# Overflow lists made in turns with the gate matrix, the last U blocks in the experts' pipeline, and the overflow pairs as the last row operations

## The chip, the cores and the metric

The kernel runs on one core of a Trainium2 chip. Its metric is the device time of one execution in microseconds (us). The engines are TensorE (PE, with PEld for its weight loads), VectorE (DVE), ScalarE (ACT), GpSimd (POOL) and SyncE (SP), which only issues transfers. Each engine works through its own list of instructions in order, and waits on semaphores for the others.

## The reference: what is computed

One encoder layer over 256 tokens of width 2048, in float32: a mix of retention and a gated recurrence, cross-attention over 256 memory tokens, then a feed-forward layer of 16384 experts of one neuron each ("PEER"), and a last normalisation. The change lies in the PEER part:

```
h = h + concat([retention, recurrence]) @ w_out
h = h + memory_cross_attention(...)
q = xn @ peer_w_q                      # 8 heads, two halves each
...                                    # top 16 of 128 keys in each half, top 16 of their 256 pairs
gate = softmax(top_sc)                 # 8 x 16 = 128 experts for each token, eid = 128*i1 + i2
act  = gelu(sum_d xn[t, d] * u_tab[eid[t, k], d])
out[t] = sum_k gate[t, k] * act[t, k] * v_tab[eid[t, k]]
```

`u_tab` and `v_tab` are 16384 x 2048 each, 134 MB a table.

## The kernel before, in words

**Dense weights.** A weight piece is 512 KB of float32, loaded by SP into `raw` (128 x 1024). ACT rounds it to `hi` (L119 or L1092), DVE subtracts to get the rest, `lo` (L120 or L1098), and PE multiplies hi by the activations' two parts and lo by one of them. So each weight piece takes one load, one ACT cast, one DVE subtraction and some 2.7 us of matmuls.

**The experts are split.** 96 x 128 experts (`RD` = 96) are computed densely, for all 256 tokens: 12 chunks (`NCH`) of 8 blocks of 128 experts. For each chunk, the U half makes the hidden values (8 blocks of two pieces, PSUM tile `U`, folded by DVE into `foldu`, gelu on ACT into `act`), a gate matrix zeroes what a token did not choose, and the V half multiplies 16 pieces into the output. The gate matrix is built by `gbuild`: for each four tokens DVE makes one-hot matrices `o` (L868, L871), ACT scales one of them with the gates (L874), PE multiplies them into `G` (L884), the result is copied to `gs` (L886), and each time 16 tokens are full, `gs` goes to DRAM as `gd` (L890, 768 KB, in pieces of 512 bytes). 64 such groups, 16 such transfers. `gs` has two buffers. Each chunk later reads its two halves of `gd` back as `raw<-gd` and multiplies (`prep`, or `prep_steps` with L1046).

**The other 32 x 128 experts are fetched by row.** `chosen` gathers, with indirect transfers of 1 MB issued by POOL (L1135), one U row or V row for each of 128 tokens into a ring of four tiles (`gat` x3 and `h[1]`). A U row is used by one DVE dot product with the normalised tokens (L1152), a V row by one DVE multiply-add into `hh` (`axpy`, L1160). 36 slots for each of the two token tiles: 72 dots and 72 axpys, three gathers ahead. `compact` (with matmuls `off` and `spill`) makes the lists. A token with more than 36 such experts has the rest in an overflow list; `spill` treats up to two of its entries (`OV`) for each partition: two gathers of U rows, two of `hn` (the normalised tokens), two dots, a one-hot matrix `oh` with the weights, two gathers of V rows, and 16 float32 matmuls of those rows with `oh` (L996). What overflows even that is worked off in `rest`, a branch that a flag guards.

**What sets the order.** Up to the sixth U chunk a scheduler orders the instructions of each engine; side work (`gbuild`, then `compact`) is fed in by a `Weave`, `wv`, which earns `rate` credits with each weight piece and spends them on the generator's steps. From there the pipeline `run(steps)` is written out by hand: raw loads six steps ahead, hi three, lo two. Its steps are V pieces, U pieces of the chunk that lies six further on (`LEAD`), and G steps (the gate product). The row operations of `chosen` are fed in by the same `Weave` at `RC`. Chunks 0 to 5 have V and U steps, chunks 6 to 10 V steps only; then `wv.drain()` issues the row operations that are left, `rest()` follows, and `v_final(11)` does the last chunk with the final normalisation.

## Time and profile before

| | |
|---|---|
| time, median of 3 runs | 2092.89 us (2092.3 to 2096.95) |
| the profiled execution: time, span | 2099.48 us, 2097.7 us |
| granted TensorE clock, mean | 0.993 |
| PE, DVE, ACT, POOL busy | 2030.7, 1698.7, 1039.0, 342.0 us |
| from DRAM, to DRAM | 541.99 MB, 18.87 MB |

The span runs from the first to the last instruction. "Busy" of PE counts stretches in which matmuls were in the array or queued for it. The profile's windows give, for any stretch, the busy time of each engine, the granted clock of TensorE and the share of time that the 16 DMA engines were busy; its lists of waits say what ended an engine's idle time; its timeline lists single instructions, runs of equal ones put together. Of this kernel's span, the stage with the gate matrix and the last scheduled U chunks ends at about 1249 us, chunks 0 to 5 of the hand-written pipeline run to about 1782 us, chunks 6 to 10 to 2038 us, and the rest is the drain, the last chunk and the output.

### The profile page before, as it was taken

To read this page: it belongs to the slowest core of one execution; us is meant where nothing else is said; L and a number is where in the kernel's file an instruction comes from. 1 tells how busy PE (TensorE), PEld (TensorE's weight loads), DVE (VectorE), ACT (ScalarE), POOL (GpSimd) and SP (SyncE) were. 2 spreads that over 40 slices of the span, in tenths; PEclk is the share of its full clock that TensorE was granted. 3 is DMA by queue.
4 is the path that set the end of the run, shared out by engine and by line. 5 is a ranking of instruction groups with operands and counts; after the bars stand their busy time and mean duration, and the time that the engine had idled before them with its cause. 6 is when DMAs were issued, how large, how long until landed. Compare 5 with 4: busy or idle time off the path is not lost.

```text
span 2097.7 us, 29005 instructions
## 1 busy us (share of the span) xinstructions
PE 2030.7 (97%) x10452; PEld 1721.0 (82%) x10452; DVE 1698.7 (81%) x2455; ACT 1039.0 (50%) x1600; POOL 342.0 (16%) x195
## 2 busy tenths in 40 slices
PE   8999999999999999999999989999999999989997
PEld 6888878888888888888889968888888888767785
DVE  6859866744554457999987779999999999989897
ACT  6565434544544455554578853444444444433334
POOL 0200021000000000000000002323333332445342
PEclk9999999999999999999999999999999999999999
DMA  8675646566654468555686579999999999999874
GB/s 283 236 233 171 218 134 184 172 191 190 184 170 141 143 188 283 170 182 179 192 275 192 171 242 371 389 382 400 362 354 358 351 378 409 375 371 391 315 263 157
DMA packets 155015, 542.92 MB, mean 259 GB/s; under 512 B 17136, under 2 KB 44400, under 8 KB 136560
## 3 DMA queue, kind: packets, MB, share of 16 engines
q1 hardware_dynamic: 132832, 400.48, 56.7%
q0 software_dynamic: 22032, 140.53, 16.9%
q8 instruction: 82, 1.34, 0.3%
q14 instruction: 69, 0.57, 0.1%
HBM read 541.99 MB, written 18.87 MB: 267 GB/s over the span
## 4 chain that ended last, share of the span: by engine, by line
PE 77%; DVE 14%; DMA 4%; issue 3%; ACT 1%; POOL 1%; ACTq 0%; DVEq 0%; SPq 0%; POOLq 0%
PE U L129 13%; PE wb L129 8%; PE U L131 7%; PE xc L171 6%; PE xc L172 6%; PE xc L174 6%; PE acc L956 5%; PE acc L953 5%; PE acc L954 5%; PE wb L131 4%; DVE lo L120 4%; PE G L884 2%; PE V L956 2%; PE V L953 2%; PE V L954 2%
## 5 line engine op out<-in xcount | busy, mean ns | idle before, releaser
L120 DVE TENSOR_TENSOR lo<-raw,hi 128x1024 fp32r<-128x1024 f32 x396 | 486.0, 1230 | 261.9 <-PE xc L174 118.8
L119 ACT CAST hi<-raw 128x1024 fp32r<-128x1024 f32 x396 | 415.3, 1050 | 301.2 <-PE xc L172 165.2
L1092 ACT CAST hi<-raw 128x1024 fp32r<-128x1024 f32 x272 | 283.9, 1049 | 265.6 <-PE acc L954 91.1
L129 PE MATMUL U<-xn,hi 128*128 128x512 f32 x1536 | 401.7, 398 | 7.8 <-ACT hi L119 6.1
L1098 DVE TENSOR_TENSOR lo<-raw,hi 128x1024 fp32r<-128x1024 f32 x272 | 328.2, 1221 | 35.0 <-issue 16.6
L129 PEld LDWEIGHTS U<-xn,hi 128*128 128x128 f32 x1536 | 277.8, 190 | 58.3 <-ACT hi L119 6.2
L1135 POOL DMA_INDIRECT gat<-in_Us_dram,idx x69 | 122.2, 1771 | 682.6 <-DVE gat L1152 424.5
L131 PEld LDWEIGHTS U<-xn,lo 128*128 128x128 f32 x1536 | 210.1, 190 | 18.3 <-DVE lo L120 2.3
L131 PE MATMUL U<-xn,lo 128*128 128x256 f32 x1536 | 218.5, 284 | 1.8 <-DVE lo L120 1.3
L1152 DVE SCALAR_TENSOR_TENSOR gat<-gat,h 128x2048 f32<-128x2048 f32 x69 | 157.7, 2285 | 0.0
L953 PE MATMUL acc<-hi,ah 128*128 128x512 f32 x384 | 150.7, 392 | 1.5 <-DVE foldu L937 1.5
L954 PE MATMUL acc<-hi,al 128*128 128x512 f32 x384 | 150.4, 392 | 0.0
L129 PE MATMUL wb<-hT,hi 128*128 128x512 f32 x448 | 119.8, 400 | 0.0
L956 PE MATMUL acc<-lo,ah 128*128 128x512 f32 x384 | 103.4, 391 | 4.9 <-DVE lo L120 3.4
L1135 POOL DMA_INDIRECT gat<-in_Vs_dram,idx x39 | 86.7, 2223 | 130.3 <-DVE hh L1160 112.7
L129 PE MATMUL wb<-xT,hi 128*128 128x512 f32 x368 | 93.4, 394 | 2.1 <-ACT hi L119 2.1
L129 PEld LDWEIGHTS wb<-hT,hi 128*128 128x128 f32 x448 | 81.3, 189 | 14.0
L1160 DVE SCALAR_TENSOR_TENSOR hh<-gat,coef,hh 128x2048 f32<-128x2048 f32 x39 | 91.5, 2346 | 0.1
L956 PEld LDWEIGHTS acc<-lo,ah 128*128 128x128 f32 x384 | 71.9, 188 | 21.8 <-DVE lo L120 4.7
L1135 POOL DMA_INDIRECT h<-in_Vs_dram,idx x33 | 70.7, 2144 | 108.3 <-DVE hh L1160 101.5
L953 PEld LDWEIGHTS acc<-hi,ah 128*128 128x128 f32 x384 | 72.5, 189 | 16.8 <-DVE foldu L937 1.8
L954 PEld LDWEIGHTS acc<-hi,al 128*128 128x128 f32 x384 | 72.6, 189 | 15.2
(411 smaller groups left out, 3654.4 us busy)
## 6 DMA issues: line engine op xcount, KB each, us to landing
raw<-in_U_dram SPq DMA_DIRECT2D x192, 512.0 KB, 4.9
raw<-in_V_dram SPq DMA_DIRECT2D x192, 512.0 KB, 7.9
raw<-in_w_xyg_dram SPq DMA_DIRECT2D x48, 512.0 KB, 4.5
raw<-in_w_qkv_dram SPq DMA_DIRECT2D x48, 512.0 KB, 4.2
raw<-in_w_xk_dram SPq DMA_DIRECT2D x32, 512.0 KB, 3.6
raw<-in_w_xv_dram SPq DMA_DIRECT2D x32, 512.0 KB, 4.2
raw<-in_w_out_dram SPq DMA_DIRECT2D x32, 512.0 KB, 4.2
raw<-in_w_xq_dram SPq DMA_DIRECT2D x32, 512.0 KB, 3.5
```

Of the source, the lines that this page charges most:

```text
L119: A.copy(hi, raw)
L120: V.tensor_tensor(lo, raw, hi.bitcast(F32), op=ALU.subtract)
L129: PE.matmul(pt, hi[:, ks], xt[:, kb, :], start=(kb == 0), stop=(kb == KB - 1))
L131: PE.matmul(pt[:, :T], lo[:, ks], xt[:, kb, :T], start=False, stop=False)
L171: PE.matmul(pt, xh, hi[:, w], start=(n == 0 and k == 0), stop=False)
L953: PE.matmul(pt, ah[:, c, t_], hi[:, w], start=(first and c == 0), stop=False)
L954: PE.matmul(pt, al[:, c, t_], hi[:, w], start=False, stop=False)
L956: PE.matmul(pt, ah[:, c, t_], lo[:, w], start=False, stop=(last and c == 7))
L1092: A.copy(his[t], raws[t])
L1098: V.tensor_tensor(los[t], raws[t], his[t].bitcast(F32), op=ALU.subtract)
L1135: G.indirect_dma_start(gat, None, a[tab], bass.IndirectOffsetOnAxis(ap=idx[tt][:, k:k + 1], axis=0), bounds_check=NS - 1, oob_is_err=False)
L1152: V.scalar_tensor_tensor(gat, gat, 1.0, h[0], op0=ALU.mult, op1=ALU.mult, accum_out=dots[tt, k0][:, k:k + 1])
```

## The change

1. `gbuild` and `compact` are fed in turns instead of one after the other (`turns`), at a rate of 2.35 instead of 1.9. Every second copy G to `gs` is made by DVE, the others by ACT (before: all by ACT). The 16 transfers `gd<-gs` are issued by POOL instead of SP. The ring's `gat` tiles are cleared by POOL at the end of `compact`, instead of by DVE later.
2. `CUT` = 2: of the sixth U chunk, only two of the eight blocks are made by `u_chunk` under the scheduler; the other 12 pieces and the first chunk's two G steps become steps 0 to 13 of the pipeline, which so has 284 weight steps instead of 272. The old `prep`, with its wave of small steps, is gone. The weave is drained before, and the two loads `hh<-hd` (1 MB each) are issued at step 8 of the pipeline.
3. The overflow pairs are no longer a side job of chunks 7 to 9. Their gathers follow the last row operations, in the same ring; the two dots come after the last axpy, the V rows are fetched after them, and the 16 matmuls are added to the last chunk: 12 to the PSUM tiles of the first three column groups, 4 to those of the last.

```
-RA, RB, RC = 1.1, 1.9, 1.17
+RA, RB, RC = 1.1, 2.35, 1.17
+CUT = 2
...
+        ring.extend(slot("ms", [P, D], f"gat{n}") for n in range(3))
+        for gat in ring:
+            G.memset(gat, 0.0)
+        ring.append(h[1])
+
+    def turns(one, two):
+        for x in one:
+            yield x
+            y = next(two, None)
+            if y is not None:
+                yield y
+        yield from two
...
-                A.copy(gs[:, :, g0:g0 + 4, :],
-                       pt[:, :4 * RD].rearrange("p (t c x) -> p c t x", t=4, x=8))
+                (V.tensor_copy if m % 2 else A.copy)(
+                    gs[:, :, g0:g0 + 4, :], pt[:, :4 * RD].rearrange("p (t c x) -> p c t x", t=4, x=8))
...
-                    nc.sync.dma_start(gd[:, :, tl, :].rearrange("q p t c -> p q t c"), gs)
+                    G.dma_start(gd[:, :, tl, :].rearrange("q p t c -> p q t c"), gs)
...
-    def u_chunk(i):
+    def u_chunk(i, blocks):
-        for c in range(8):
+        for c in blocks:
-            if i == LEAD - 1 and c == 2:
-                while "gbuild" not in done:
-                    wv.pump(3.0)
-                wave.append(prep(0))
-        flush()
...
         for t, step in enumerate(steps):
+            if t == 8:
+                for tt in range(TT):
+                    nc.sync.dma_start(hh[tt], hd[tt])
...
-    def chosen(blocks):
+    def chosen(blocks, tail=False):
+        extra = [lambda: fetch(next_gat(), a["Us"], NS, spl["i"][:, 0:1]),
+                 lambda: spill_x(1, next_gat()),
+                 lambda: fetch(next_gat(), a["Us"], NS, spl["i"][:, 1:2])] if tail else []
         for m in range(len(tasks) + AHEAD):
             if m < len(tasks):
                 f, tab, tt, k0, n, k = tasks[m]
                 held.append(rows(tab, tt, k0 + k))
+            elif extra:
+                held.append(extra.pop(0)())
...
+                    if tail and not dots_left:
+                        spill_x(0, h[0])
                 yield 2.2
+        if tail:
+            spill_dot(0, held[-3], h[0])
+            spl["v"] = [next_gat() for b in range(OV)]
+            yield 2.2
+            spill_dot(1, held[-1], held[-2])
+            yield 2.2
+            spill_rows()
+            spill_weights()
...
-    wv.add(gbuild())
-    wv.add(compact())
+    wv.add(turns(gbuild(), compact()))
...
-        u_chunk(i)
+        u_chunk(i, range(8 if i < LEAD - 1 else CUT))
+    wv.drain()
...
-    wv.add(chosen(blocks_of(0, 0, BASE) + blocks_of(1, 0, BASE)))
-    steps = []
+    wv.add(chosen(blocks_of(0, 0, BASE) + blocks_of(1, 0, BASE), True))
+    steps = woven(list(u_steps(LEAD - 1))[2 * CUT:], prep_steps(0), 6, 3)
```

**Where gate matrix and U chunk end, on PE.** G is a group of four tokens of the gate matrix, U a piece of the dense U half, `off` and `spill` are `compact`'s. Before:

```order
L884 MATMUL G<-o_10820,o_10818 128x96 x4
L884 MATMUL G<-o_10834,o_10832 128x96 x4
L884 MATMUL G<-o_10849,o_10847 128x96 x4
L884 MATMUL G<-o_10864,o_10862 128x96 x4
L884 MATMUL G<-o_10878,o_10876 128x96
L798 MATMUL off<-ct,tri 128x1
L799 MATMUL off<-ct,ones 128x1
L800 MATMUL off<-ct,tri 128x1
L884 MATMUL G<-o_10878,o_10876 128x96 x3
L831 MATMUL spill<-sel,own 128x12
L129 MATMUL U<-xn,hi 128x512 x7
L831 MATMUL spill<-sel,own 128x12
```

After, the last groups of G, and what follows them:

```order
L896 MATMUL G<-o_10949,o_10947 128x96 x2
L130 MATMUL U<-xn,hi 128x512
L896 MATMUL G<-o_10949,o_10947 128x96 x2
L132 MATMUL U<-xn,lo 128x256 x8
L130 MATMUL U<-xn,hi 128x512
L896 MATMUL G<-o_10963,o_10961 128x96 x2
L130 MATMUL U<-xn,hi 128x512
L896 MATMUL G<-o_10963,o_10961 128x96 x2
L130 MATMUL U<-xn,hi 128x512 x5
L132 MATMUL U<-xn,lo 128x256 x8
L130 MATMUL U<-xn,hi 128x512 x9
L132 MATMUL U<-xn,lo 128x256 x8
```

The stretch of G groups without U pieces between them is gone, and `compact`'s matmuls stand further ahead.

**The gate matrix's transfers, at the same place.** Before, on SP, `gd<-gs` among the U loads, and the first two loads of the gate matrix:

```order
L890 DMA gd<-gs 128x12x128
L112 DMA raw<-gd 128x1024
L112 DMA raw<-in_U_dram 128x1024
L890 DMA gd<-gs 128x12x128
L112 DMA raw<-in_U_dram 128x1024 x2
L890 DMA gd<-gs 128x12x128 x5
L1326 DMA hh_11282<-hd 128x2048
L890 DMA gd<-gs 128x12x128
L112 DMA raw<-gd 128x1024
L112 DMA raw<-in_U_dram 128x1024 x4
```

After, on POOL, from the clearing of the ring on (the gathers L1099 are row operations; the second one into `gat_9629` is the fifth gather):

```order
L856 MEMSET gat_9631 128x2048
L1099 DMA gat_9629<-in_Us_dram,idx 128x2048
L902 DMA gd<-gs 128x12x128
L1099 DMA gat_9630<-in_Us_dram,idx 128x2048
L1099 DMA gat_9631<-in_Us_dram,idx 128x2048
L1099 DMA h_4211<-in_Us_dram,idx 128x2048
L902 DMA gd<-gs 128x12x128 x14
L1099 DMA gat_9629<-in_Us_dram,idx 128x2048
L902 DMA gd<-gs 128x12x128
```

And after, on DVE, from the last copy to `gs` (L898) up to the second gate product (L1007), which needs the last of those transfers (L1116 is the dot, L987 the fold of a U block):

```order
L898 COPY gs<-G 128x12x32
L1059 TENSOR_TENSOR lo<-raw_11005,hi 128x1024
L987 TENSOR_TENSOR foldu<-U,foldu 128x256
L1059 TENSOR_TENSOR lo<-raw_11006,hi 128x1024
L1116 SCALAR_TENSOR_TENSOR gat_9630,dots<-gat_9630,h_4210 128x2048
L1007 TENSOR_TENSOR act_7481<-raw,act_7481 128x8x128
L987 TENSOR_TENSOR foldu<-U,foldu 128x256
L1059 TENSOR_TENSOR lo<-raw,hi 128x1024
L1116 SCALAR_TENSOR_TENSOR gat_9631,dots<-gat_9631,h_4210 128x2048
L1059 TENSOR_TENSOR lo<-raw,hi 128x1024
L987 TENSOR_TENSOR foldu<-U,foldu 128x256
L1007 TENSOR_TENSOR act_7481<-raw,act_7481 128x8x128
```

The last transfer of the gate matrix now stands on POOL behind a gather that waits for the first dot, which stands on DVE right ahead of the last copy; and the gate product that needs that transfer follows on DVE eleven rows behind the copy. Before, the transfer was SP's, behind nothing but loads.

**The drain, on DVE.** Before, from the last lo of the pipeline on (L1160 is the axpy, L120 the lo of the last chunk):

```order
L1098 TENSOR_TENSOR lo<-raw_11314,hi 128x1024
L1160 SCALAR_TENSOR_TENSOR hh_11283<-gat_11292,coef,hh_11283 128x2048
L120 TENSOR_TENSOR lo<-raw,hi 128x1024
L1160 SCALAR_TENSOR_TENSOR hh_11283<-gat_11293,coef,hh_11283 128x2048
L1230 TENSOR_REDUCE more<-fl 128x1
L1160 SCALAR_TENSOR_TENSOR hh_11283<-gat_11294,coef,hh_11283 128x2048
L1232 CAST many<-more 128x1
L120 TENSOR_TENSOR lo<-raw,hi 128x1024
L1160 SCALAR_TENSOR_TENSOR hh_11283<-h_4211,coef,hh_11283 128x2048
```

Four more axpys follow in turns with four more lo, up to the branch. After (L1124 axpy, L1195 the overflow pairs' dots, L121 the lo of the last chunk, L1205 their one-hot weights):

```order
L1124 SCALAR_TENSOR_TENSOR hh_10983<-gat_9631,coef,hh_10983 128x2048
L1059 TENSOR_TENSOR lo<-raw,hi 128x1024
L1124 SCALAR_TENSOR_TENSOR hh_10983<-h_4211,coef,hh_10983 128x2048
L1195 SCALAR_TENSOR_TENSOR gat_9629,od<-gat_9629,h_4210 128x2048
L1195 SCALAR_TENSOR_TENSOR gat_9631,od<-gat_9631,gat_9630 128x2048
L1217 TENSOR_REDUCE more<-fl 128x1
L121 TENSOR_TENSOR lo<-raw,hi 128x1024
L1200 TENSOR_TENSOR od<-od,spg 128x2
L1219 CAST many<-more 128x1
L121 TENSOR_TENSOR lo<-raw,hi 128x1024
L1205 TENSOR_SCALAR oh<-iota,spt,od 128x128 x2
```

One axpy instead of eight stands behind the pipeline's last lo; behind it two dots stand between the pipeline's last lo and the first lo of the last chunk, and the second of them reads a row whose gather can only be issued when the axpy into which `gat_9631` goes is done.

More of the change, by code (lines that the diff above doesn't have):

```diff
@@ L821, in compact @@
         spl["i"] = tp.tile([P, OV], I32, tag="spi", name="spi")
-        spl["g"] = tp.tile([P, 40], F32, tag="spg", name="spg")[:, :OV]
+        spl["g"] = tp.tile([P, 64], F32, tag="spg", name="spg")[:, :OV]
         for b in range(OV):
@@ L893, in gbuild @@
         done.add("gbuild")
[L895 to L928 removed]
+    ahs, spare = {}, {}
+    def u_chunk(i, blocks):
         act = acts[i] = tp.tile([P, 8, T], F32, tag="act", name=f"act{i}", bufs=LEAD)
[L930 removed]
+        for c in blocks:
             pt = mm("U") if i or c else pt0
@@ L961, in v_unit @@
         first, last = not kept or i == 0, not kept or i == NCH - 1
-        late = i == SPILL + 2
+        late = i == NCH - 1
         for q in range(4):
@@ L984, in products @@
                 if not box:
-                    if i == SPILL + 2:
-                        while side:
-                            for _ in side.pop():
-                                pass
                     box.extend(acc[dc] if kept else (mm("V0"), mm("V1")))
                 ah, al = ahs[i]
-                late = i == SPILL + 2
-                v_mms(ah, al, hi, lo, q, list(enumerate(box)), not kept or i == 0, not kept and not late)
-                if late and q == 3:
-                    for tt in range(TT):
-                        for b in range(OV):
-                            PE.matmul(box[tt], spl["oh"][:, b, tt * P:(tt + 1) * P],
-                                      spl["v"][b][:, dc * 512:(dc + 1) * 512], start=False,
-                                      stop=(not kept and b == OV - 1))
+                v_mms(ah, al, hi, lo, q, list(enumerate(box)), not kept or i == 0, not kept)
             def added(dc=dc, kept=kept, box=box):
@@ L1177, in chosen @@
         held = []
+        dots_left = sum(t[0] is dot for t in tasks)
+        extra = [lambda: fetch(next_gat(), a["Us"], NS, spl["i"][:, 0:1]),
+                 lambda: spill_x(1, next_gat()),
+                 lambda: fetch(next_gat(), a["Us"], NS, spl["i"][:, 1:2])] if tail else []
         for m in range(len(tasks) + AHEAD):
@@ L1222, in spill, with spill_rows @@
                 V.tensor_scalar(spl["t"][:, bs], spl["t"][:, bs], -float(P), None, op0=ALU.add)
-        yield
-        done.add("spill")
+    def spill_rows():
+        for b in range(OV):
+            fetch(spl["v"][b], a["Vs"], NS, spl["i"][:, b:b + 1])
     def rest():
@@ L1276, in v_final @@
             for q in range(4):
-                v_mms(ah, al, vl[:, q, 0], vl[:, q, 1], q, [(tt, pt)])
+                v_mms(ah, al, vl[:, q, 0], vl[:, q, 1], q, [(tt, pt)], last=False)
+            for b in range(OV):
+                PE.matmul(pt, spl["oh"][:, b, tt * P:(tt + 1) * P], spl["v"][b][:, ds], start=False,
+                          stop=(b == OV - 1))
             V.tensor_tensor(hh[tt][:, ds], hh[tt][:, ds], pt, op=ALU.add)
@@ L1318, in hybrid_layer_kernel @@
     done.add("pb")
-    wv.add(gbuild())
-    wv.add(compact())
+    wv.add(turns(gbuild(), compact()))
     wv.rate = RB
     for i in range(LEAD):
-        u_chunk(i)
+        u_chunk(i, range(8 if i < LEAD - 1 else CUT))
+    wv.drain()
     hh = [slot("qs", [P, D], f"hh{tt}") for tt in range(TT)]
-    for tt in range(TT):
-        nc.sync.dma_start(hh[tt], hd[tt])
-    wv.drain()
     pg.__exit__(None, None, None)
@@ L1333, in hybrid_layer_kernel @@
     pct = pc.__enter__()
-    ring = [slot("ms", [P, D], f"gat{n}") for n in range(3)] + [h[1]]
-    for gat in ring[:3]:
-        V.memset(gat, 0.0)
     pj = tc.tile_pool(name="pj", bufs=1, space=bass.MemoryType.PSUM)
```

83 lines of the change are left out of this document (22 added, 61 removed).

## The prediction

> **What bounds the kernel now.** I read the page's head and its chain first:
>
> ```profile
> span 2097.7 us, 29005 instructions
> PE 2030.7 (97%) x10452; PEld 1721.0 (82%) x10452; DVE 1698.7 (81%) x2455; ACT 1039.0 (50%) x1600; POOL 342.0 (16%) x195
> PE 77%; DVE 14%; DMA 4%; issue 3%; ACT 1%; POOL 1%; ACTq 0%; DVEq 0%; SPq 0%; POOLq 0%
> ```
>
> PE is busy in 97% of the span, so all that can be won without removing matmuls is 2097.7 - 2030.7 = 67 us of idle time and what the clock takes; and the change removes no matmul. So I looked for the places where PE stands, with the windows (length, busy time of PE, PEld, DVE, ACT, POOL, then the granted clock, the DMA share and GB/s):
>
> ```profile
> 1155.00:1209.00 54.00, 54.00 (x386) 50.18 (x384) 42.57 (x65) 48.06 (x142) 0.00 (x0) 1.00 0.56 173
> 1209.00:1220.00 11.00, 8.14 (x58) 7.18 (x58) 8.02 (x25) 10.36 (x33) 0.00 (x0) 1.00 0.51 146
> 1220.00:1249.00 29.00, 21.45 (x114) 18.63 (x114) 20.32 (x50) 12.81 (x19) 0.00 (x0) 0.82 0.86 318
> 1249.00:1782.00 533.00, 530.86 (x2683) 450.96 (x2682) 514.13 (x535) 235.19 (x303) 171.53 (x97) 1.00 0.96 371
> 1782.00:1826.00 44.00, 41.70 (x184) 33.60 (x183) 43.82 (x46) 19.48 (x21) 16.84 (x7) 1.00 0.95 371
> 1826.00:1900.00 74.00, 63.72 (x263) 49.39 (x262) 64.12 (x64) 22.11 (x23) 33.57 (x15) 0.98 0.95 381
> 1900.00:2038.00 138.00, 133.39 (x553) 103.15 (x553) 128.40 (x117) 53.66 (x56) 62.06 (x26) 1.00 0.87 321
> 2038.00:2062.00 24.00, 20.59 (x82) 15.81 (x81) 23.75 (x18) 7.29 (x10) 7.90 (x4) 0.93 0.56 184
> ```
>
> Four places count: the end of the gate matrix and of the scheduled U chunks (1209 to 1249, 10.4 us idle, clock down to 0.82), the V chunks without U (1782 to 2038, 17.2 us idle), the drain (3.4 us idle, clock 0.93), and, as a place that is full, chunks 0 to 5 (2.1 us idle in 533, so PE sets the pace, with DVE at 96% and DMA at 0.96 right behind). The waits name what PE stood for, up to 1782 us, and then from there on:
>
> ```profile
> PE U L129 <- ACT hi L119: 6.1, 1, 6.1
> PE spill L831 <- DVE own L817: 1.9, 1, 1.9
> PE acc L953 <- DVE foldu L937: 1.5, 1, 1.5
> ```
>
> ```profile
> PE acc L956 <- DVE lo L1098: 10.6, 10, 4.3
> PE acc L956 <- DVE lo L120: 3.4, 3, 2.2
> PE V L953 <- ACT hi L1092: 2.4, 3, 1.0
> ```
>
> The first three are the end of the gate matrix; lo L1098 is the V chunks, lo L120 the drain. Between 1826 and 1872 us ACT in its turn waits for the loads:
>
> ```profile
> ACT hi L1092 <- DMA raw<-in_V_dram: 19.9, 7, 5.2
> ```
>
> That is the chunk in which the overflow pairs' six 1 MB gathers run beside the row operations.
>
> **Step 1, the end of the gate matrix.** From 1209 to 1249 PE was busy for 8.14 + 21.45 of 40 us: 10.4 idle. Some matmuls behind the gaps were slow:
>
> ```profile
> 1220.01 3.06 PE L129 MATMUL U<-xn,hi 128*128 128x512 f32 x7
> 1233.93 3.70 PE L129 MATMUL U<-xn,hi 128*128 128x512 f32 x8 [6.08 <-ACT hi L119]
> 1238.41 1.78 PE L129 MATMUL U<-xn,hi 128*128 128x512 f32 x7
> ```
>
> Seven take 1.78 us at full clock, so the first row lost 1.3 us and the second 3.70 - 2.03 = 1.7. Excess of the stretch: 10.4 + 3.0 = 13.4 us. All of it hangs on the order that goes: G groups with no U pieces between, the lists behind them, then U pieces held by the first gate product. After, G and lists run among U pieces and the stage ends in the pipeline: -13.4.
>
> The Trainium skill, "TensorE: Matmul & The Clock Gate", Part 1 (The HAM clock gate), says that an idle window of about 3.4 us halves the clock and that as much sustained work restores it; the row after the 6.08 us gap agrees (8 matmuls at 3.70 us for 2.03). By it every new gap of that size would cost up to 1.7 us beyond its own length, and gaps of 1 or 2 us nothing; that would leave the sum where it is.
>
> What comes instead: the last `gd<-gs` stands on POOL behind the fifth gather, which waits for the first dot; the second gate product needs it, by way of SP's `raw<-gd`, which also holds the raw loads behind it. Prices:
>
> ```profile
> L886 ACT COPY gs<-G 128x384 f32<-128x384 f32 x64 | 29.8, 471 | 3.3 <-PE G L884 3.0
> L1135 POOL DMA_INDIRECT gat<-in_Us_dram,idx x69 | 122.2, 1771 | 682.6 <-DVE gat L1152 424.5
> 814.64 0.75 POOL L673 DMA_DIRECT2D hn<-h  x1 [485.63 <-DVE h L671]
> 817.23 0.57 POOL L673 DMA_DIRECT2D hn<-h  x1 [1.84 <-DVE h L671]
> gd<-gs SPq DMA_DIRECT2D x16, 768.0 KB, 5.3
> raw<-gd SPq DMA_DIRECT2D x24, 512.0 KB, 8.1
> L890 SPq DMA_DIRECT2D gd<-gs x16: 359/377/426, 1076.3 to 1218.5; - x16
> L1098 DVE TENSOR_TENSOR lo<-raw,hi 128x1024 fp32r<-128x1024 f32 x272 | 328.2, 1221 | 35.0 <-issue 16.6
> L1152 DVE SCALAR_TENSOR_TENSOR gat<-gat,h 128x2048 f32<-128x2048 f32 x69 | 157.7, 2285 | 0.0
> L1046 DVE TENSOR_TENSOR act<-raw,act 128x1024 f32<-128x1024 f32 x22 | 47.2, 2144 | 0.0
> 1780.80 0.41 DVE L1026 TENSOR_TENSOR foldu<-U,foldu 128x256 f32<-128x256 f32 x1
> ```
>
> No direct transfer of many small pieces is issued by POOL before. `hn<-h` has 128 rows of 8 KB and took POOL 0.57 and 0.75 us; `gd<-gs` has 12 x 128 = 1536 pieces. The issue lies between 0.6 us (nothing for a piece) and 9 us (12 times 0.75); I take 3, in the lower half, because 0.6 for 128 pieces must hold a fixed part. The chain from the last copy: 0.5 + 1.8 for the gather + 3 + 5.3 to land + 8.1 for the load back = 18.7 us (16.3 to 24.7). DVE's cover in the order: four lo, two dots, one gate product and three folds of 0.41, that is 4 x 1.22 + 2 x 2.29 + 2.14 + 1.2 = 12.8. DVE so waits some 6 us; lo is made up to two pieces ahead, which PE needs 5.4 us for (2.72 each, step 3), but the raw loads behind SP's wait come late too, and a slow clock may follow. I take +4.5, with 0 (a lead that holds) and 15 (24.7 - 12.8, and slow clock) as ends. Before that, 32 copies of 0.47 us move from ACT (89% busy at 1155 to 1209) to DVE (79%) and the feed is 2.35/1.9 = 1.24 times as dense: 15 us more in some 150 is 10% of DVE, besides denser one-hots, so DVE comes near 95% and will make PE wait a little. +1 (0 to 8; nothing if the six-deep buffers carry it). The memsets are hidden: POOL is idle there (0.00 in the first three windows). SP's 16 issues of 0.38 us gone: 0, SP was no releaser.
>
> **Step 2, U pieces into the pipeline.** The 12 U pieces and two gate products cost PE the same there as under the scheduler (a stage in which PE was busy for 530.86 of 533 us): 0. But 12 more steps of 1.17 credits feed 14 credits, at 2.2 for a row operation 6.4 of them, before the pipeline's end; the order shows one axpy behind the last lo where eight stood. The two `hh` loads: 2 MB among loads at 0.96 DMA share, six pieces ahead: 0.
>
> **Step 3, the overflow pairs.** The V chunks 6 to 10 have 80 pieces:
>
> ```profile
> 1996.64 1.07 PE L956 MATMUL acc<-lo,xe 128*128 128x512 f32 x4
> 1999.36 1.07 PE L956 MATMUL acc<-lo,xe 128*128 128x512 f32 x4
> L996 PE MATMUL acc<-spl,oh 128*128 128x512 f32 x24 | 10.8, 592 | 0.0
> L996 PE MATMUL V<-spl,oh 128*128 128x512 f32 x8 | 3.6, 592 | 0.0
> ```
>
> One piece is 2.72 us, 80 are 217.6; with 14.4 of overflow matmuls 232.0, and the stage took 256: excess 24. What goes: 1826 to 1900 has 74 - 63.7 = 10.3 idle and 0.02 x 74 = 1.5 of clock, 11.8. What stays: the first chunk, without overflow work, has DVE busy for 43.82 of 44 us and PE idle for 2.3; 74 us of that kind make 3.9. So 7.9 go with the six gathers and two dots. Of 24 - 17.2 = 6.8 us that no window names (pieces at a slower pace) I give the change 3, its share of the idle time. Together -11. Ends: -4.6, the two dots' DVE time alone, and -20, if DVE, started earlier, keeps its lead in all five chunks. The 14.4 of matmuls move to the last chunk: 0.
>
> The drain pays. Its parts:
>
> ```profile
> 2055.42 2.34 DVE L1160 SCALAR_TENSOR_TENSOR hh<-h,coef,hh 128x2048 f32<-128x2048 f32 x1
> gat<-in_Us_dram,idx POOLq DMA_INDIRECT x69, 9.4
> ```
>
> Before, PE idled 3.4 us there and lost 0.07 x 24 = 1.7 to the clock: 5.1. After, the second pair's U row can be gathered only when the axpy on `gat_9631` is done. Behind that axpy DVE has a lo (1.2), an axpy (2.3) and the first dot (2.3), so it is free for the second dot after 5.8 us, while the row lands after 9.4, or 13 with the gathers ahead of it in the queue. DVE waits 3.6 to 7.2, does the dot (2.3) and then the lo on which all of the last chunk hangs (1.2): from the pipeline's last lo to that one 11.8 to 15.3 us. PE has up to two pieces in hand (5.4) and the next hi part (1.8), so it stands for 5 to 8 us, and for 13 with nothing in hand; with a slow clock behind it, 10. Against 5.1: +5 (-5 to +10). The V rows go into tiles that are free after that axpy and the first dot, land 9.4 us later, and are first read behind four more pieces of PE (11 us) past the lo above; the one-hot weights are five short DVE operations in the same time: hidden. If that cover went, each us would show.
>
> **Sum.** -13.4 + 4.5 + 1 - 11 + 5 = -13.9 us: span 2097.7 to 2083.8. The profiled execution took 2099.48, 0.3% above the median of 2092.89, within the spread of the three (to 2096.95), so I take the difference off the median: 2079 us.
>
> **The rivals.**
>
> *POOL as a bottleneck (slower).* `gs` has two buffers. The 16 transfers were issued from 1076.3 to 1218.5, one in 9.5 us, and a buffer is filled, issued and landed in turn. With 9 us of issue and 5.3 to land, two buffers give a period of (9.5 + 9 + 5.3)/2 = 11.9 us: 15 x 2.4 = 36 us more for the gate matrix, DVE and ACT held at their copies and PE with them. That decides when issue and landing together pass 9.5 us, so from an issue of about 4.2 us on. Time then: 2079 + 36 = 2115 at the full price, 2097 at half of it. For it: the count of pieces, and gathers of 128 rows that take 1.77 us in the mean when DVE is busy, three times the direct transfer of as many. Against it: the 0.6 us must hold a fixed part. The Trainium skill bears on this from both sides. "SBUF — State Buffer" (SBUF: two separate sides) says that a transfer issued by POOL has its descriptors written by that engine, and that a VectorE operation in a two-port mode, such as a float32 copy from SBUF to SBUF, locks it out; the new copies read PSUM, so by its letter they would not, and no run here shows such an issue yet. "DMA: Bandwidth & Descriptors" (Anatomy of one DMA) calls descriptor generation "small, variable": by that the issue would be near 1 us, the stall in step 1 nearer 2 us, and the time 2077.
>
> *The drain and the last gate product wait longer (no change).* Both new waits at their ends, 15 and 10 us, in place of 4.5 and 5: -13.4 + 15 + 1 - 11 + 10 = +1.6; half-way between, -6. For it: DMA at 0.95 and more beside the gathers, so that landings stretch; both waits sit on engines on whose queue everything else waits. Against it: the six pieces of raw lead. Time: 2087 to 2095.
>
> *DVE keeps its lead (a larger gain).* If the row operations, which start 12 pieces earlier, leave DVE ahead when the U pieces end, the five chunks give 20, and the waits are 2 and 2: -13.4 + 2 + 0 - 20 + 2 = -29: 2064. Against it: 43.82 of 44 us busy where nothing disturbed it.
>
> *The lists' waits only move.* `compact` in turns with `gbuild` could carry its waits (1.9 us on `own`, and DVE's share of the 6.1) among the U pieces; then step 1 gives 7 and not 13.4, time 2085. For it: ACT at 89% there. It lies within the forecast's own range.
>
> **How the numbers follow.** The measurement tells about 0.2% (4 us) from no change. Forecast, 2070 to 2088 with the last rival in it: 0.49. Larger gain, 2062 to 2070: 0.15. No change by the two waits, 2089 to 2097: 0.16. POOL as a bottleneck, above 2097: 0.20. So faster 0.64, same 0.16, slower 0.20. The range from 2064 to 2098 leaves out some 0.18 above and 0.02 below; the forecast's own is 2070 to 2088.
>
> **What would show it.** Step 1: `gd<-gs` on POOL at 1 to 4 us each, sixteen of them evenly spaced, PE busy for all but 5 us through the 60 us around the pipeline's start, ACT and DVE both near 90% before it. Wrong if POOL is busy for 7 us and more with each, or DVE's wait for `raw<-gd` passes 10 us. Step 3: no wait of PE above 2 us in the V chunks, their stage near 256 - 14.4 - 11 = 231 us for 80 pieces; wrong if lo is still the releaser for 15 us and more. Drain: one wait of PE for the first lo of the last chunk, 5 to 8 us, ended by the second overflow dot and its gather; then full clock and the same output stage as before. The prediction is wrong as a whole if the stage before 1209 us grows by more than 10 us.

## The result, and the profile after

| | before | after |
|---|---|---|
| time, median of 8 runs | 2093.89 us (2090.22 to 2098.95) | 2105.78 us (2099.25 to 2108.46) |
| ratio, with 95% interval | | 1.0051 (1.0035 to 1.0066) |
| the profiled execution: time, span | 2099.48, 2097.7 us | 2102.2, 2100.4 us |

The kernel became slower by 0.5%, where 2079 us and a gain of 0.7% were forecast; the measured time lies outside the range of 2064 to 2098. The profiled execution of before took longer than the median of its kernel and that of after less, so the two traces differ by 2.7 us where the medians differ by 11.9. The traces are therefore read by stages, each from its own start. Four marks stand in every trace: the first matmul of the expert selection's scores, after its wait near 897 to 901 us (nothing of the change lies ahead of it), the first matmul of V, the first one of V in chunk 7, and the first one of the last chunk. Times between them, from the rows of the timeline, in us:

| | selection to first V | first V to chunk 7's first V | from there to the last chunk | last chunk to end | sum |
|---|---|---|---|---|---|
| before | 347.6 | 580.9 | 209.1 | 59.2 | 1196.8 |
| after | 360.1 | 581.5 | 184.8 | 76.6 | 1203.0 |
| after, with the 14.4 us of overflow matmuls put back | 360.1 | 581.5 | 199.2 | 62.2 | 1203.0 |
| difference | +12.5 | +0.6 | -9.9 | +3.0 | +6.2 |
| forecast | -7.9 | 0 | -11 | +5 | -13.9 |

The head of the page, after, shows the same share of PE as before:

```profile
span 2100.4 us, 28984 instructions
PE 2028.1 (97%) x10452; PEld 1721.9 (82%) x10452; DVE 1703.1 (81%) x2484; ACT 1030.7 (49%) x1570; POOL 378.1 (18%) x214
```

The stage that lost, in windows (length, busy time of PE, PEld, DVE, ACT, POOL, granted clock, DMA share, GB/s), first before, then after:

```profile
1000.00:1050.00 50.00, 49.08 (x278) 42.36 (x276) 49.63 (x112) 28.38 (x47) 0.00 (x0) 1.00 0.60 187
1050.00:1100.00 50.00, 48.71 (x313) 43.95 (x314) 43.12 (x83) 37.27 (x90) 4.36 (x4) 1.00 0.81 279
1200.00:1260.00 60.00, 49.59 (x287) 43.42 (x286) 44.40 (x102) 35.84 (x83) 1.73 (x1) 0.91 0.68 235
```

```profile
1000.00:1050.00 50.00, 44.16 (x258) 37.57 (x257) 49.97 (x118) 27.99 (x54) 4.77 (x3) 1.00 0.48 144
1050.00:1100.00 50.00, 45.04 (x288) 40.56 (x287) 38.05 (x110) 28.68 (x69) 6.31 (x6) 0.93 0.74 258
1200.00:1260.00 60.00, 45.48 (x271) 39.64 (x270) 47.90 (x71) 30.02 (x66) 13.78 (x9) 0.91 0.77 285
```

Two places lost. From 1000 to 1100 us PE idled 2.2 us before and 10.8 after, and part of it now runs at a lower clock (0.93, some 3.5 us). From 1200 to 1260 us, where 13.4 us were to be won, PE idles 14.5 instead of 10.4 us. Taken from the selection to the first V, each trace from its own marks, PE's idle time grows from 12.6 to 23.8 us. The waits of PE from 990 to 1262 us, after:

```profile
PE U L130 <- ACT hi L1053: 8.8, 1, 8.8
PE U L130 <- DVE foldu L987: 3.7, 2, 3.2
PE G L896 <- ACT o L886: 3.6, 1, 3.6
PE U L132 <- DVE lo L121: 2.8, 5, 1.5
PE acc L929 <- DVE al L1025: 2.0, 1, 2.0
PE rT L751 <- DVE rt L735: 1.8, 1, 1.8
```

The first is the hand-over to the pipeline. Its cause is on the queue of the loads; SP's own waits from 1200 to 1262 us, then POOL's gather and transfer, DVE's gate product and the U load that ACT waited for:

```profile
SPq L1048 <- PE G L896: 27.2, 2, 26.8
SPq L1048 <- DMA gd<-gs: 13.8, 1, 13.8
```

```profile
1219.48 1.06 POOL L1099 DMA_INDIRECT gat<-in_Us_dram,idx  x1 [6.96 <-DVE gat L1116]
1220.54 1.06 POOL L902 DMA_DIRECT2D gd<-gs  x1
1238.00 2.00 DVE L1007 TENSOR_TENSOR act<-raw,act 128x1024 f32<-128x1024 f32 x1 [3.80 <-DMA raw<-gd]
1243.03 2.11 ACT L1053 CAST hi<-raw 128x1024 fp32r<-128x1024 f32 x2 [8.38 <-DMA raw<-in_U_dram]
1244.12 3.78 PE L130 MATMUL U<-xn,hi 128*128 128x512 f32 x8 [8.75 <-ACT hi L1053]
```

The last transfer of the gate matrix stands behind the fifth gather. That gather waited 6.96 us for the first dot, but only until 1219.48 us, when the last copy, done at 1219.67, was still running; so the order of issue cost the transfer about 1 us. What made it late is the time from issue to landing, 12.9 us, the longest of the sixteen (least, median, most):

```profile
DMA to landing us min/median/max: 4.9/5.5/12.9
```

SP stood 13.8 us for it, and it was not DVE's 3.80 us for `raw<-gd` that PE felt but the U loads queued behind SP's wait: 8.75 us of idle time, then eight matmuls at 3.78 us for 2.03. PE's 3.2 us for a fold, just ahead of that, came from another wait of SP: it stood 26.8 us for a matmul of the gate matrix before it issued two U loads at 1216.93 us, and ACT, which copies for the fold only after its cast, stood 3.55 us for the first of them.

The V chunks gave nearly what was forecast, and the drain cost somewhat less; the waits of PE from 1262 us to the end, after:

```profile
PE acc L931 <- DVE lo L121: 7.1, 1, 7.1
PE V L931 <- DVE lo L1059: 6.4, 5, 4.3
```

All of the drain is one wait, which ends with the last chunk's first lo; DVE's rows say why:

```profile
2023.67 2.31 DVE L1195 SCALAR_TENSOR_TENSOR gat<-gat,h 128x2048 f32<-128x2048 f32 x1
2029.40 2.29 DVE L1195 SCALAR_TENSOR_TENSOR gat<-gat,gat 128x2048 f32<-128x2048 f32 x1 [3.42 <-DMA gat<-in_Us_dram,spi]
2031.69 1.22 DVE L121 TENSOR_TENSOR lo<-raw,hi 128x1024 fp32r<-128x1024 f32 x1
```

### The profile page after: what moved, and what is told of

It reads as the page before. It is cut to its first block, busy times and chain, and to the rows that moved or that the text cites. A ratio compares the mean times of both kernels' runs of the same rounds, so it can differ in the third digit from the quotient of the medians.

```text
span 2100.4 us, 28984 instructions
## 1 busy us (share of the span) xinstructions
PE 2028.1 (97%) x10452; PEld 1721.9 (82%) x10452; DVE 1703.1 (81%) x2484; ACT 1030.7 (49%) x1570; POOL 378.1 (18%) x214
## 4 chain that ended last, share of the span: by engine, by line
PE 78%; DVE 11%; DMA 5%; issue 3%; POOL 2%; ACT 1%; ACTq 0%; POOLq 0%; DVEq 0%; SPq 0%
PE U L130 14%; PE U L132 7%; PE wb L130 7%; PE xc L172 6%; PE xc L173 6%; PE xc L175 6%; PE acc L931 5%; PE acc L929 5%; PE acc L928 5%; PE wb L132 4%; DVE lo L121 3%; PE G L896 2%; PE V L931 2%; PE V L928 2%; PE V L929 2%
## 5 line engine op out<-in xcount | busy, mean ns | idle before, releaser
L121 DVE TENSOR_TENSOR lo<-raw,hi 128x1024 fp32r<-128x1024 f32 x384 | 469.1, 1224 | 250.0 <-PE xc L175 118.7
L120 ACT CAST hi<-raw 128x1024 fp32r<-128x1024 f32 x384 | 402.5, 1050 | 300.2 <-PE xc L173 164.9
L1099 POOL DMA_INDIRECT gat<-in_Us_dram,idx x69 | 129.5, 1877 | 251.3 <-DVE gat L1116 230.7
L1116 DVE SCALAR_TENSOR_TENSOR gat<-gat,h 128x2048 f32<-128x2048 f32 x69 | 157.8, 2287 | 0.0
L1099 POOL DMA_INDIRECT gat<-in_Vs_dram,idx x39 | 82.5, 2115 | 115.2 <-DVE hh L1124 102.0
L1099 POOL DMA_INDIRECT h<-in_Vs_dram,idx x33 | 82.7, 2507 | 110.6 <-DVE hh L1124 102.2
L1124 DVE SCALAR_TENSOR_TENSOR hh<-gat,coef,hh 128x2048 f32<-128x2048 f32 x39 | 91.7, 2352 | 0.0
```

Source lines behind the costliest of these rows:

```text
L120: A.copy(hi, raw)
L121: V.tensor_tensor(lo, raw, hi.bitcast(F32), op=ALU.subtract)
L1099: G.indirect_dma_start(gat, None, a[tab], bass.IndirectOffsetOnAxis(ap=idx[tt][:, k:k + 1], axis=0), bounds_check=NS - 1, oob_is_err=False)
L1116: V.scalar_tensor_tensor(gat, gat, 1.0, h[0], op0=ALU.mult, op1=ALU.mult, accum_out=dots[tt, k0][:, k:k + 1])
```

## The experiments

Each of the twelve kernels below ran in five rounds against the kernel before; ratios are to it, with 95% intervals. The runs of one kernel spread over 5 to 19 us, so kernels of different sittings are compared by their ratios to the kernel before; a difference of 0.001 in the ratio is 2.1 us.

**Part 3 alone, and the change without part 2.** `e1_tail_only` is the kernel before with the overflow pairs as last row operations; `e2_no_cut` is the changed kernel with the sixth U chunk and the first gate products back under the scheduler.

```
# e1: before, with chosen(..., tail=True), spill_dot, spill_rows, spill_weights and the 16 matmuls in v_final
# e2: after, with
-        u_chunk(i, range(8 if i < LEAD - 1 else CUT))
+        u_chunk(i)                                     # and the old prep, wave, tick, flush
-    steps = woven(list(u_steps(LEAD - 1))[2 * CUT:], prep_steps(0), 6, 3)
+    steps = []
```

> The kernel before with part 3 alone (overflow pairs as last row operations; feeding, gate-matrix transfers and the sixth U chunk as before). Theory: the stall in the V chunks came from the overflow gathers, and the loss of the whole change sits ahead of the first V chunk. Then the V chunks give back 11 us and the drain costs about 2 to 5: 2085 to 2088 us, ratio 0.996 to 0.9975. Rival: the V chunks gained from the 12 earlier steps of row operations (part 2), not from the overflow pairs. Then eight axpys and two dots stand in the drain, and the time is 2094 to 2099.

> The changed kernel with part 2 undone (the sixth U chunk and the first gate products under the scheduler again). Theory: of the loss ahead of the first V chunk, about 11 us sit at the start of the gate matrix (1000 to 1100 us: gathers and first lists crowd the U loads) and 5 at the hand-over to the pipeline. The first stays: from the change's 2105 the time falls by 5 to 8, to 2097 to 2100. Rival: all of the loss is the hand-over into the hand-written pipeline: 2090 or less. Second rival: the pipeline's earlier start is worth more than the hand-over costs: over 2108.

Measured: e1 2115.78 us, ratio 1.0113 (1.0092 to 1.0134); e2 2119.03 us, ratio 1.0124 (1.0103 to 1.0144). Neither expectation held, theory or rival: both are slower by far than the change itself. The trace of e1 shows one reason that has nothing to do with order: in its V chunks each matmul whose weights are `ah` or `al` started 0.234 us after the last in the mean over many, where the kernel before has 0.227. (The weights are the 128x128 part of the operands; what streams past them is 512 columns of `hi` or `lo`.) In e1 and e2 these two tiles start 32 bytes above a multiple of 64. It is not `hi`: in the same trace, chunks 7 to 10 stream `hi` past weights in another tile, `xe`, and are not slower. The rows give count, busy time and mean ns of one:

```profile
L960 PE MATMUL acc<-hi,ah 128*128 128x512 f32 x240 | 95.2, 396 | 0.0
L960 PE MATMUL acc<-hi,xe 128*128 128x512 f32 x160 | 62.3, 389 | 0.0
```

The address was tested alone:

```
# f1: before, with
-        spl["g"] = tp.tile([P, 40], F32, tag="spg", name="spg")[:, :OV]
+        spl["g"] = tp.tile([P, 48], F32, tag="spg", name="spg")[:, :OV]
# f2: e1, with spg at 40 columns
```

> The kernel before with nothing changed but the width of one small tile (spg, 40 columns made 48), which moves the tiles behind it, ah and al among them, by 32 bytes, from a multiple of 64 to 32 above one. In the runs with part 3 alone and without part 2 they lay so too, and a matmul that streams ah or al took 0.234 us where the kernel before takes 0.227. Theory: the address alone does it; 112 V pieces of 2.72 us take 2.81, and the last chunk's 16 as well: 11 to 12 us, 2104 to 2106, ratio 1.005 to 1.006. Rival: those matmuls were slow for another reason (what runs beside them); then this kernel takes 2093 as before.

> The kernel before with part 3 alone once more, with spg at 40 columns, so that ah and al lie as in the kernel before. Theory: the V chunks give back 9 us; the drain, with eight axpys and two dots behind the pipeline's last lo and a late one-hot weight, costs 14 more than before: 2098 to 2104. Rival: the address was not the cause; it stays at 2115. Second rival: part 3 is a gain by itself, as forecast: 2085 to 2088.

Measured: f1 2103.55 us, ratio 1.0051 (1.0035 to 1.0068). Eight unused columns cost 11 us. In the mean over 640 such matmuls of each trace the starts are 0.2267 us apart before and 0.2329 in f1. The two kernels' rows, before and then f1:

```profile
1349.13 0.39 PE L953 MATMUL V<-hi,ah 128*128 128x512 f32 x1
1349.35 0.39 PE L954 MATMUL V<-hi,al 128*128 128x512 f32 x1
1349.58 0.39 PE L953 MATMUL V<-hi,ah 128*128 128x512 f32 x1
```

```profile
1349.22 0.40 PE L953 MATMUL V<-hi,ah 128*128 128x512 f32 x1
1349.45 0.40 PE L954 MATMUL V<-hi,al 128*128 128x512 f32 x1
1349.68 0.40 PE L953 MATMUL V<-hi,ah 128*128 128x512 f32 x1
```

The tiles' start in a partition is 201024 in the kernel before, a multiple of 64, and 201056 in f1. The changed kernel's 201280 is a multiple of 64 again, because it widened spg to 64 columns; so the change does not suffer from this, but e1 and e2 did. The weight loads themselves take 188 ns in both kernels; why the matmuls follow each other more slowly is not shown. e2 was not run again at the old address.

f2 took 2105.61 us, ratio 1.0056 (1.0037 to 1.0075), just above the 2098 to 2104 expected: part 3 by itself is a loss of 12 us. Its stages are 348.4, 580.9, 185.0 and 89.7 us: the V chunks gain 9.7 us net of the 14.4, as in the changed kernel, and the drain loses 16.1. PE's waits there:

```profile
PE acc L963 <- DVE lo L121: 11.1, 3, 9.1
PE acc L977 <- DVE oh L1234: 6.1, 1, 6.1
```

So part 3 needs part 2: without the 12 early pieces eight axpys stand in the drain, the dots come later still, and even the one-hot weights are waited for.

**The lists in turns.** `e3_no_turns`:

```
-    wv.add(turns(gbuild(), compact()))
+    wv.add(gbuild())
+    wv.add(compact())
```

> The changed kernel with gbuild first and compact after it, everything else of the change kept. Theory: the lists in turns are what brings the four gathers and the lists' chain into the start of the gate matrix; without turns the 10 us of idle time at 1000 to 1100 us fall to 3, and the lists' waits of some 4 to 6 us come back at the end: 2099 to 2103. Rival: the turns are harmless and the denser feed (2.35) makes the idle time: 2105 to 2112.

Measured: 2092.19 us, ratio 0.9992 (0.9978 to 1.0006), 12 us better than the change by the ratios and 13.6 by the medians: more than expected. From selection to first V it takes 346.0 us for the change's 360.1, nearly all of the difference. Without turns, the gathers come only after the tenth gate-matrix transfer, and the last transfer stands ahead of the fifth gather, so that this one edit takes both causes away: the window 1050 to 1100 is at 48.89 us of PE, and the 8.75 us gap at the hand-over is gone.

**The last transfer, and the early gathers, each alone.** `e4_gd_last_sp` and `f4_late_gathers`, both on the changed kernel with turns:

```
# e4
-                    G.dma_start(gd[:, :, tl, :].rearrange("q p t c -> p q t c"), gs)
+                    (nc.sync if m == T // 4 - 1 else G).dma_start(gd[:, :, tl, :].rearrange("q p t c -> p q t c"), gs)
# f4: e4, with the ring cleared at the end of gbuild, and there
+            G.tensor_copy(gat[:, :1], gs[:, 0, 15, :1])
```

> The changed kernel with the last of the 16 gate-matrix transfers issued by SP instead of POOL, so that it no longer stands behind the fifth gather. Theory: the 8.8 us gap at the hand-over is that transfer's late landing, with the U loads held behind SP's wait for it; the gap falls to 3 or less and its slow clock of 1.7 goes: 2095 to 2098. Rival: SP is held there by the two new raw buffers, whose memory the gate matrix frees last; then nothing changes: 2103 to 2107.

> The changed kernel with turns kept, the last gate-matrix transfer on SP (2100 us), and the first four row gathers held back until the gate matrix is done (the ring's tiles are touched by POOL then). Theory: the stall of PE at 1055 to 1075 us is four gathers and a gate-matrix transfer issued within 6 us ahead of the U loads; without them the stretch 1050 to 1100 has under 2 us of idle time (4 to 5 before), while the first dots come late and may cost up to 10 us at the hand-over. Rival: the lists' chain of small operations on DVE, PE and ACT makes the stall; then 1050 to 1100 keeps its 4 to 5 us.

Measured: e4 2100.04 us, ratio 1.0035 (1.0023 to 1.0048): better than the change by 3 us by the ratios, whose intervals overlap, and by 5.7 by the medians, a little less than expected. The trace is clearer: the stage to first V falls from 360.1 to 352.9, and the gap of 8.75 us is gone. SP issued the transfer at 1221.33 us, just after POOL had issued the same gather (1221.11), and could issue the load that needs it at 1226.65: 5.3 us where POOL's queue took 12.9. On POOL the transfer landed 2 us after the gather ahead of it (issued at 1219.48, landed 12.0 us later); on SP it landed more than 4 us before the same gather (1221.11 and 10.0). So the place behind a 1 MB gather in the same queue made it land late. The rival holds in part: SP's wait of 26.8 us for the gate matrix is still there, ACT stands 3.74 us for the U load issued after it, and PE 3.43 us for the fold behind that, with eight matmuls at 3.75 us after it. f4 took 2108.77 us, ratio 1.0082 (1.0054 to 1.011). Its windows:

```profile
1000.00:1050.00 50.00, 44.16 (x259) 37.71 (x258) 49.97 (x117) 27.77 (x53) 3.62 (x2) 1.00 0.47 141
1050.00:1100.00 50.00, 50.00 (x335) 45.31 (x334) 45.26 (x123) 34.89 (x87) 3.82 (x4) 1.00 0.67 209
1200.00:1260.00 60.00, 39.87 (x226) 34.16 (x226) 41.89 (x55) 22.21 (x46) 15.81 (x14) 0.86 0.87 339
```

The middle stretch is full: the stall at 1050 to 1100 does not come without the four gathers, 4 MB, which the changed kernel issues between 1048.8 and 1055.3 us together with the first gate-matrix transfer, ahead of the U loads. f4 keeps the lists' chain in its place, so the rival is out. ACT, after, then waits for one of them:

```profile
1061.79 1.04 ACT L120 CAST hi<-raw 128x1024 fp32r<-128x1024 f32 x1 [6.08 <-DMA raw<-in_U_dram]
```

Held back, they come late at the hand-over instead, as expected, and cost more there: one wait of 13.1 us. The first stretch is not touched by them.

**The rate.** `g1_rb19`:

```
-RA, RB, RC = 1.1, 2.35, 1.17
+RA, RB, RC = 1.1, 1.9, 1.17
```

> The changed kernel with the feed rate of before (1.9 instead of 2.35), turns and all else kept. Theory: the 5.8 us of PE idle at 1000 to 1050 us (0.9 before the change) come from the denser feed of the gate matrix's one-hots beside the selection that already fills DVE; they fall to 2 or less, and the last groups of the gate matrix then stand alone at the end again, for 5 to 8 us: 2100 to 2108. Rival: the lists in turns, not the rate, fill DVE there; then 1000 to 1050 keeps its 5 us.

Measured: 2128.59 us, ratio 1.0132 (1.0101 to 1.0163), far above the 2100 to 2108 expected, though the window that it was made for went as the theory says:

```profile
1000.00:1050.00 50.00, 49.65 (x279) 42.53 (x279) 49.93 (x116) 28.30 (x47) 2.94 (x2) 1.00 0.62 191
1050.00:1100.00 50.00, 50.00 (x322) 45.20 (x320) 42.71 (x93) 30.95 (x68) 7.78 (x7) 1.00 0.78 275
1100.00:1186.00 86.00, 86.00 (x589) 79.06 (x588) 70.06 (x142) 61.87 (x168) 7.16 (x7) 1.00 0.52 159
1186.00:1245.00 59.00, 46.07 (x201) 42.86 (x200) 35.72 (x66) 32.94 (x113) 7.26 (x7) 0.53 0.35 104
```

The second window qualifies what f4 showed. g1 issues the same four gathers there, between 1048.9 and 1060.7 us, and ACT stands 4.05 us for a U load, yet PE is full. So early gathers alone do not make PE stand; in the changed kernel they came with a gate-matrix transfer within 6.5 us, and after a stretch in which the denser feed had already made PE wait. Which of the two decides was not tested.

Two rows of PE's timeline in the last window:

```profile
1196.68 3.73 PE L896 MATMUL G<-o,o 128*128 128x96 f32 x16 [0.84 <-ACT o L886]
1201.26 3.73 PE L896 MATMUL G<-o,o 128*128 128x96 f32 x16 [0.84 <-ACT o L886]
```

With 84 pieces instead of 96 and the lists in between, the old rate does not bring the gate matrix to its end: from 1186 to 1245 us the groups stand alone, and PE, although after a first gap of 2.27 us it idles for only 0.84 us at a time, is granted 0.53 of its clock. So the old rate is too low once part 2 has taken pieces away, and the price of the higher one is the 5 us at 1000 to 1050, where DVE was at 49.63 of 50 us already. (e1 and f2, with the old rate and all 96 pieces, idle 1.3 and 0.2 us there.)

**The drain.** `f3_no_turns_tailfix` is e3 with the dots of the overflow pairs as two of the row operations, four and nine places behind the last regular dot, their U rows fetched three operations ahead in the ring, and the tokens' rows of both in `h[0]`, one after the other; the V rows follow as the last two fetches.

```
+            items.insert(last + 4, ("s", 0))
+            items.insert(last + 9, ("s", 1))
+            items += [("v", b) for b in range(OV)]
...
+                if it[0] == "s":
+                    spill_dot(it[1], held[m - AHEAD], h[0])
```

> The changed kernel without turns (2092 us) and with the overflow pairs' two dots placed among the last nine axpys, each one's rows fetched three row operations ahead, instead of behind all of them. Theory: the 7.1 us wait of PE for the first lo of the last chunk is the second dot's gather, which cannot be issued before the last axpys; with it goes the slow clock: 2083 to 2086. Rival: the two dots' gathers only come late elsewhere, or the tokens' rows, which now share one tile, hold DVE: 2089 to 2094.

Measured: 2088.65 us, ratio 0.9976 (0.9965 to 0.9987), some 3 us better than e3: about half of the gain expected. The wait for the last chunk's first lo fell from 7.1 to 4.1 us, and not to nothing. DVE's rows of f3 in front of it:

```profile
2009.77 1.23 DVE L1059 TENSOR_TENSOR lo<-raw,hi 128x1024 fp32r<-128x1024 f32 x1
2010.90 2.29 DVE L1205 SCALAR_TENSOR_TENSOR h<-h,h 128x2048 f32<-128x2048 f32 x1
2013.11 2.36 DVE L1124 SCALAR_TENSOR_TENSOR hh<-gat,coef,hh 128x2048 f32<-128x2048 f32 x1
2015.84 2.35 DVE L1124 SCALAR_TENSOR_TENSOR hh<-gat,coef,hh 128x2048 f32<-128x2048 f32 x1
2018.23 1.22 DVE L121 TENSOR_TENSOR lo<-raw,hi 128x1024 fp32r<-128x1024 f32 x1
```

No row has a wait any more, but a dot and two axpys, 7.0 us of DVE, still stand between the pipeline's last lo and the next, 8.5 us apart. So of the 7.1 us some 3 were the gather's lateness, and 4.1 are DVE work that stands there in this order too.

**Three kernels on f3, in one sitting.** `g3_f3_gdsp` gives the gate-matrix transfers back to SP; `g4_f3_actcopy` gives the copies `gs<-G` back to ACT; `g5_f3_uncut` takes part 2 away, and keeps `ah` and `al` at a multiple of 64 bytes.

```
# g3
-                    G.dma_start(gd[:, :, tl, :].rearrange("q p t c -> p q t c"), gs)
+                    nc.sync.dma_start(gd[:, :, tl, :].rearrange("q p t c -> p q t c"), gs)
# g4
-                (V.tensor_copy if m % 2 else A.copy)(
+                A.copy(
# g5: the old prep, wave, tick and flush, spg at 40 columns, and
-        u_chunk(i, range(8 if i < LEAD - 1 else CUT))
+        u_chunk(i)
-    steps = woven(list(u_steps(LEAD - 1))[2 * CUT:], prep_steps(0), 6, 3)
+    steps = []
```

> The best version so far (no turns, the overflow pairs' dots among the last axpys: 2088.7 us) with all 16 gate-matrix transfers issued by SP, as before the change. Theory: POOL's issue is cheap (1.02 us each) and SP's is too; the time stays within 2 us, 2086 to 2091. Rival: SP's loads of U come late behind the waits of these transfers, 2093 or more. Second rival: POOL's part in the gate matrix delays the row gathers, and without it 2084 or less.

> The best version so far with all 64 copies of the gate matrix to gs on ACT, as before the change (half are on DVE). Theory: ACT, 79 to 87% busy from 1100 to 1200 us, goes to 87 to 95%, and a few more waits for its casts appear: 2089 to 2092. Rival: DVE is the engine that is late there, and the time falls to 2085 or less.

> The best version so far with part 2 undone: the sixth U chunk and the first gate products stay under the scheduler, so that the row operations start 12 pieces later (spg at 40 columns, so that ah and al keep their address). Theory: the 12 early steps are worth about 6 row operations in the drain; without them seven axpys and a dot stand there again and the first gate product waits as before: 2096 to 2102. Rival: the hand-over to the hand-written pipeline costs as much as the early steps give: 2087 to 2091.

g3: 2091.65 us (2086.87 to 2095.04, and one run of 4089.24 that nothing here explains), ratio 0.9973 (0.9958 to 0.9988), the same as f3's 0.9976, as the theory says. What the engine that issues pays, in the rows of that line, after and then g3 (duration in ns, least, median and most; first and last start):

```profile
L902 POOL DMA_DIRECT2D gd<-gs x16: 1018/1020/1093, 1050.2 to 1220.5; - x16
```

```profile
L902 SPq DMA_DIRECT2D gd<-gs x16: 377/377/639, 1046.3 to 1197.0; - x16
```

POOL pays 1.02 us, SP 0.38, and the time does not tell them apart here, where no gather stands right ahead of the last transfer.

g4: 2085.88 us (2083.54 to 2090.41), ratio 0.9949 (0.9931 to 0.9967): faster than the kernel before by 0.5%, and the fastest of all, below the 2089 to 2092 expected and close to the rival's 2085. The stage to the first V takes 343.2 us, f3's 346.0. The windows, f3 and then g4:

```profile
1050.00:1100.00 50.00, 48.91 (x339) 44.84 (x338) 43.94 (x72) 41.59 (x118) 5.53 (x6) 1.00 0.69 213
1100.00:1200.00 100.00, 99.45 (x682) 91.41 (x682) 87.19 (x172) 78.96 (x215) 15.45 (x14) 1.00 0.77 253
```

```profile
1050.00:1100.00 50.00, 50.00 (x348) 46.19 (x347) 46.76 (x106) 46.08 (x130) 12.04 (x10) 1.00 0.87 310
1100.00:1200.00 100.00, 100.00 (x685) 92.15 (x684) 72.71 (x121) 86.75 (x232) 10.24 (x10) 1.00 0.70 216
```

PE is full in both with the copies on ACT, although ACT is the busier engine then (92% in the first window); with half of them on DVE it stood for the one-hots, 1.6 us in these two windows. The stage gives 2.8 us, but the two traced runs as wholes take the same (2086.4 and 2086.6 us); the rest of the 5.8 us to g3's median is not located, and the intervals of g4 and g3 overlap. That the copies belong on ACT is therefore likely, and not shown.

g5: 2098.1 us, ratio 1.0014 (1.0001 to 1.0026), as expected: part 2 is worth 8 us beside f3 by the ratios, 9.5 by the medians. Without it the drain has these waits:

```profile
PE acc L968 <- DVE lo L121: 8.9, 1, 8.9
PE acc L965 <- ACTq L1265: 5.9, 1, 5.9
```

## Why the prediction was wrong, step by step

**Step 1, the denser feed and the lists: one of the two terms that failed.** It was set at +1 (0 to 8). From 1000 to 1100 us PE idles 8.6 us more than before, and a clock of 0.93 in the second half costs 3.5 more: 12. That is the sign by which the prediction called itself wrong as a whole, over 10 us more ahead of 1209. The forecast took DVE's load from 1155 to 1209 us (79%), where the feed ends; where it starts, from 1000 to 1050, DVE had 0.37 us of 50 to spare before, a window that was not looked at. g1, with the old rate, has no loss there (0.35 us idle), and e3, with the new rate and without turns, has 4.4 us idle: that part is the rate. The other part is the turns' burst on top of it, which f4 took away: four gathers of 1 MB and a transfer within 6.5 us, ahead of U loads; at the old rate (g1) the gathers cost PE nothing. The working counted POOL's time for the memsets, and of the moved gathers neither the bytes nor what they stand in front of.

**Step 1, the hand-over: the other term that failed; its chain was named rightly, its victim and its parts were not.** From the end of the last copy to the gate product 18.2 us were forecast (18.7 with the copy); 1219.67 to 1238.00, 18.3 us, were measured. That the sums agree is luck: gather, issue and landing took 13.8 us where 1.8 + 3 + 5.3 = 10.1 were added up, because the transfer landed 12.9 us after its issue, and the load back took 4.3 us for 8.1. DVE waited 3.8 us for 6 forecast. But PE lost 8.75 us and 1.7 of clock, because SP stood 13.8 us for `gd<-gs` and the U loads were queued behind it. The prediction named this ("the raw loads behind SP's wait come late too") and gave it no price of its own. Idle time there, to be cut by most of 10.4 us, became 14.5. e4 removed only the queue place of the last transfer and got 3 us back by the ratios, 7.2 in its trace's stage. The gain of 13.4 us was too large by itself: it took all of that excess to hang on the order that goes. In no kernel did the stage to the first V fall by more than 4.4 us (343.2 in g4), and even without turns (e3) waits of 2.3, 2.2 and 3.0 us stand at the hand-over.

**"The lists' waits only move"** was a rival worth 6 us. Turns did cost, and more: 12 us as a whole by the ratios (e3). But the waits are not the lists' own, since f4 keeps the lists' place and is full from 1050 to 1100; they are those of what came with the lists, the early gathers and the last transfer's place behind the fifth.

**POOL as a bottleneck** stopped at its first condition: 1.02 us of issue where 4.2 was the point of decision. The time came out above 2097 all the same, for another reason; the 0.20 for it was not a forecast of this. By the Trainium skill's "DMA: Bandwidth & Descriptors" (Anatomy of one DMA), which calls descriptor generation "small, variable", the issue was put near 1 us; the 16 rows agree. The lock-out that the Trainium skill's "SBUF — State Buffer" (SBUF: two separate sides) describes was not seen at these 16 issues, with half of the copies on DVE reading PSUM, as its letter says.

**Step 2** was costed at 0 with a remark on earlier row operations. The stage from the first V to chunk 7 kept its time (+0.6). What it gives is in the drain: g5, without it, ends its trace with 88.4 us from the last chunk where f3 has 73.2, and is 8 us behind f3 as a whole by the ratios. The forecast had this inside step 3's drain term and V chunks and not as a gain of step 2; the sum is not touched by that.

**Step 3, the V chunks:** -11 forecast, -9.9 measured; f2, part 3 alone, has -9.7. The sign "no wait above 2 us" failed: five waits for lo, 6.4 us, are left, the longest 4.3. **The drain:** +5 forecast, +3.0 measured, by the mechanism named: one wait, 7.1 us (5 to 8 forecast), ended by the second dot behind its gather.

**What stays open.** The stages of the two traces differ by 6.2 us and the medians by 11.9; the traced run of before lay above its kernel's median and that of after below its own, and no stage can be named for the rest. What the early gathers cost in time as a whole is not shown: f4, made for that, lost at the hand-over what it won before, so it only shows the place. And with part 2 no kernel was without the 5 us at 1000 to 1050 and also finished the gate matrix in time; g1 did the first and missed the second.

## What to carry to other kernels

When work is interleaved earlier, look at the window in which it will land and not at the one from which it comes: an engine with 0.4 us of 50 free has no room, whatever it has 100 us later. Count moved DMAs as bytes in front of the loads that feed the bound engine, and for a load queue that waits on a round trip through DRAM count everything queued behind the wait; that, not the waiting engine's own idle time, is the price. Price such a transfer by the gathers that are under way with it: behind one gather in the same queue it landed after 12.9 us, where the median was 5.5. When an experiment removes tiles, keep the addresses of the rest, or a shift of 32 bytes will be taken for an effect of the order.
